# One product for B u, four groups' y beside each other on TensorE's columns, and B turned a layer earlier

## The chip, the cores and the metric

The kernel runs on one core of a Trainium2 chip. The metric is the device time of one execution in microseconds (us), the median of three runs. One execution was also taken by the hardware profiler; its trace is what the rows below come from. TensorE is called PE in rows, VectorE DVE, ScalarE ACT, GpSimd POOL, SyncE SP; PEld is TensorE's weight load.

## The reference, cut to what matters

Two blocks run one after the other: a two-layer attention block over 256 latent and 256 context tokens, and then a block with a state-space mixer (S5), a latent attention (MLA) and a feed-forward part. The change touches the S5 mixer and the tables that it needs. There are 64 groups of 16 channels and 64 complex states; the sequence has 272 tokens, and the outputs of the last 258 are used.

```python
b_bar = ((lam_bar - 1.0) / lam)[..., None] * b
bu = jnp.einsum('blgc,gpc->blgp', uf.astype(jnp.complex64), b_bar)
a = jnp.broadcast_to(lam_bar, bu.shape)
_, h = lax.associative_scan(combine, (a, bu), axis=1)   # h_t = lam_bar h_(t-1) + bu_t
y = jnp.real(jnp.einsum('blgp,gcp->blgc', h, c))
y = y + d_skip * uf
g = jax.nn.gelu(y)
out = g * jax.nn.sigmoid(g @ w_glu + b_glu)
```

## The kernel before

Two groups are one step n of 32: their 2 x 64 states fill 128 partitions. Activations lie transposed, channels on partitions and tokens along the free dimension. A float32 product of accuracy is made of three: `mm3` multiplies a high and a low part of the weights (`wh`, `wl`, both float32r) with a high and a low part of the activations. A stream of weight units (`W`, 512 KB each as a rule) feeds everything: SP loads `raw` (three buffers), ACT rounds it to `wh` (L313), DVE makes `wl` (L327), TensorE multiplies 24 times per unit (4 chunks, 2 halves, 3 products). Work that goes beside the stream is written as Python generators that advance at fixed places of a unit, `pre` and `post`; so the order on each engine's queue is fixed when the program is built, and each engine works its queue in that order.

`s5()` is such a generator. It runs beside three stretches of the stream: the input projection of the second block (`in2`, weights `win2`), the heads of the latent attention (`qb_pair`, `kv_pair`, `mla_head`; there the units are short and have plain float32 products), and the output projection `ob`. One step n is: six float32r products `bu` (L464 to L466: `mm3` for the real and the imaginary part, 32 rows of B, 272 columns) into two PSUM banks; on DVE `rotate` (L1776 to L1781: the two products with the table `e`, a sum, a difference and two scans); on POOL two products with `e` (L1784), a sum and a difference (L1785, L1786), result `pr`; and, three steps later (`late`), two float32 products `y` (L1837), each C of 128 x 128 (zero but for 32 columns) times `pr`. A step's trailing products come 32 channels at a time, and four steps share one PSUM bank; after the fourth, `gelu` follows (L1796 to L1809) on DVE and ACT. For each step SP loads `e` (two buffers) and `ct` (four buffers). Once per four steps B is loaded (`bd`), turned by two transposes (`turned_b`, L1816) and split into `bTH` and `bTL`; those take two `pre`/`post` places of their own.

The tables `etab` and `btab` lie in DRAM; `s5_tables()` makes them beside the second layer of the first block (lines 920 to 1038), and must end before the second block's memory is given out.

Of the kernel before, what the change touches and what calls it, by code (L numbers as in the profile page):

```python
# [63 lines left out]
PACE = {"in2": 6, "heads": 2, "ob": 6, "late": 3}  # L64
# [54 lines left out]
def _layout2(i):  # L119
# [43 lines left out]
    ct = np.zeros((32, 128, 2, 128), np.float32)  # L163
    for v, key in enumerate(("c_re_2", "c_im_2")):
        c = i[key][0]
        for gr in range(64):
            n, h = gr // 2, gr % 2
            o = 32 * (n % 4) + 16 * h
            ct[n, 64 * h:64 * h + 64, v, o:o + 16] = c[gr].T
# [75 lines left out]
def program(ctx: ExitStack, tc: tile.TileContext, A, stop=None):  # L245
# [294 lines left out]
    btab = dram.tile([2, 128, 32, 32], F32, name="btab")  # L540
# [346 lines left out]
    def s5_tables():  # L887
# [83 lines left out]
        for i in range(2):  # L971
# [7 lines left out]
            for v, op in enumerate((SUB, ADD)):  # L979
# [7 lines left out]
                P.dma_start(out=btab[v, :, n0:n0 + 16, :].rearrange("p n c -> p (n c)"), in_=o.rearrange("p n g c -> p (n g c)"))  # L987
# [767 lines left out]
    def s5():  # L1755
        yield
        bT = [mt_("bTH", [128, 2, 128], F32R), mt_("bTL", [128, 2, 128], F32R)]
# [8 lines left out]
        def load_b(j):  # L1766
            t = mw.tile([128, 2, 128], F32, tag="bd", name="bd", bufs=1)
            SY.dma_start(out=t, in_=btab[:, :, 4 * j:4 * j + 4, :].rearrange("v p n c -> p v (n c)"))
            return t

        def rotate(n, bu, e):
# [10 lines left out]
            o, o_ = (ring(t, 2 * NT, k).rearrange("p (v t) -> p v t", v=2) for t, k in (("pr0", 3), ("pr", 1)))  # L1782
            for x, w in ((o, co), (o_, si)):
                P.tensor_tensor(out=x, in0=g, in1=w.unsqueeze(1).to_broadcast([128, 2, NT]), op=MUL)  # L1784
# [7 lines left out]
        def gelu(j, yps):  # L1792
            y, w = ring("gy", NQ, 1), ring("gw", NQ, 1)

            def a():
                V.scalar_tensor_tensor(out=y, in0=uF(j), scalar=dsk[:, j:j + 1], in1=yps[:, 14:NT], op0=MUL, op1=ADD)  # L1796
# [16 lines left out]
        def turned_b(bd, tag):  # L1813
            pt = ps_(tag)
            for v in range(2):
                T.transpose(pt[:, v * 128:v * 128 + 128], bd[:, v, :], ident)  # L1816
            yield
            split(bT[0], bT[1], pt[:, :256].rearrange("p (v q) -> p v q", v=2))

        nxt, bd = load(0), load_b(0)  # L1820
        yield
        yield from turned_b(bd, "O")
        bd = load_b(1)
        yield
        while "x" not in R:
            yield
            yield
        late = deque()
        yps = [None]

        def late_y():
            n, c, parts = late.popleft()
            i = n % 4
# [486 lines left out]
```

## Time and profile before

| what | value |
|---|---|
| median of three runs | 2983.74 us (2981.06 to 2984.47) |
| the profiled execution's own time | 2980.39 us |
| its span | 2978.6 us |
| mean granted TensorE clock | 0.97 |
| second layer of the first block, from the tables' start | 1320 to 1766 us of the span |
| first step of S5 to the first products of the heads | 1826.5 to 1939 us |
| the heads | 1939 to 2068 us |
| fourteen units of `ob` with the last five steps of S5 | 2068 to 2139 us |

The profiled execution lies 3.4 us under the median, 1.8 us of its time outside its span. In the tables of stretches below, an engine's figure is the time in which it had an instruction in work; PEclk is the granted TensorE clock as a share of 2.4 GHz (0.5 is its lower level, 1.2 GHz, so 0.89 is a mixture of both levels). A plain float32 matmul has two records in the trace, a float32r matmul one.

### The profile page before, as it was taken

What the parts mean: (1) busy time and instruction counts of PE and PEld (TensorE: products, weight loads), DVE (VectorE), ACT (ScalarE), POOL (GpSimd) and SP (SyncE); (2) the same over time, 40 slices, a digit from 0 to 9 for tenths busy, and PEclk for the clock granted to TensorE, in tenths of its full rate; (3) what the DMA queues carried; (4) which work ended last, traced back from release to release, by engine and by line L of the source; (5) the groups of instructions that cost most, each with busy time, mean ns of one, the idle gap of its engine ahead of it and who ended that gap; (6) DMA issues with size and microseconds to landing.
All of it is one profiled execution on the core that took longest, in us unless ns stands there. A gap on an engine that the chain in (4) does not pass through costs nothing. (4 is left out here: it accounts for less than half of the span.)

```text
span 2978.6 us, 48955 instructions
## 1 busy us (share of the span) xinstructions
PE 2798.6 (94%) x19022; PEld 2530.3 (85%) x19022; DVE 1980.7 (66%) x3709; ACT 1279.2 (43%) x2196; POOL 526.1 (18%) x501
## 2 busy tenths in 40 slices
PE   6999999998999978999998988899999999999998
PEld 2677878887777978899898987866899999999998
DVE  2377667676676588766676887876865555455544
ACT  2444434244442445534345544234354444344443
POOL 0001100001111161100001125655431110011100
PEclk9999999998999989999999999898999999999999
DMA  9754454543446645534433564432455655666554
GB/s 364 259 163 134 120 150 147 171 130 119 121 139 187 220 155 192 174 100 147 141 125 115 161 191 144 132 110 84 144 160 183 183 183 180 186 187 183 182 176 156
DMA packets 176441, 483.97 MB, mean 162 GB/s; under 512 B 20944, under 2 KB 32848, under 8 KB 176208
## 3 DMA queue, kind: packets, MB, share of 16 engines
q1 hardware_dynamic: 171312, 468.62, 50.2%
q0 software_dynamic: 2880, 9.96, 0.9%
q8 instruction: 149, 2.44, 0.3%
q10 hardware_dynamic: 2016, 2.25, 0.2%
q14 instruction: 84, 0.69, 0.1%
HBM read 468.71 MB, written 12.06 MB: 161 GB/s over the span
## 5 line engine op out<-in xcount | busy, mean ns | idle before, releaser
L327 DVE TENSOR_TENSOR wl<-raw,wh 128x1024 fp32r<-128x1024 f32 (+2 forms) x650 | 809.3, 1250 | 440.5 <-ACT wh L313 435.9
L313 ACT CAST wh<-raw 128x1024 fp32r<-128x1024 f32 (+2 forms) x650 | 669.7, 1036 | 918.1 <-PE mm L465 557.1
L464 PE MATMUL mm<-nH,wh 128*128 128x512 f32 (+1 forms) x2048 | 705.5, 344 | 10.6 <-ACT kp L1109 6.7
L465 PE MATMUL mm<-nL,wh 128*128 128x512 f32 (+1 forms) x2048 | 698.0, 341 | 4.5 <-DVE nL L1097 4.5
L466 PE MATMUL mm<-nH,wl 128*128 128x512 f32 (+1 forms) x2048 | 697.0, 340 | 3.2 <-DVE wl L327 3.1
L464 PEld LDWEIGHTS mm<-nH,wh 128*128 128x128 f32 x2048 | 390.5, 191 | 62.0 <-ACT kp L1109 7.1
L465 PEld LDWEIGHTS mm<-nL,wh 128*128 128x128 f32 x2048 | 390.5, 191 | 50.8 <-DVE nL L1097 6.3
L466 PEld LDWEIGHTS mm<-nH,wl 128*128 128x128 f32 x2048 | 389.8, 190 | 50.7 <-DVE wl L327 4.0
L464 PE MATMUL mm<-ZA,wh 128*128 128x258 f32 (+1 forms) x1408 | 400.4, 284 | 5.0 <-DVE oa L1898 5.0
L466 PE MATMUL mm<-ZA,wl 128*128 128x258 f32 (+1 forms) x1408 | 399.8, 284 | 0.0
L465 PE MATMUL mm<-ZB,wh 128*128 128x258 f32 (+1 forms) x1290 | 363.8, 282 | 0.0
L669 DVE SCALAR_TENSOR_TENSOR acc<-mraw,cs,acc 128x512 f32<-128x512 f32 x420 | 295.6, 754 | 45.8 <-DMA mraw<-in_wmod 43.8
L464 PEld LDWEIGHTS mm<-ZA,wh 128*128 128x128 f32 x1408 | 267.4, 190 | 5.2 <-issue 5.2
L466 PEld LDWEIGHTS mm<-ZA,wl 128*128 128x128 f32 x1408 | 267.4, 190 | 0.0
L465 PEld LDWEIGHTS mm<-ZB,wh 128*128 128x128 f32 x1290 | 245.2, 190 | 0.0
L370 PE MATMUL mm<-wh,nH 128*128 128x256 f32 x736 | 212.5, 289 | 6.7 <-ACT nH L1533 3.4
L372 PE MATMUL mm<-wh,nL 128*128 128x256 f32 x736 | 211.0, 287 | 1.6 <-DVE nL L1535 1.5
L371 PE MATMUL mm<-wl,nH 128*128 128x256 f32 x736 | 210.2, 286 | 0.0
L464 PE MATMUL mm<-yH,wh 128*128 128x256 f32 x688 | 193.5, 281 | 0.0
L465 PE MATMUL mm<-yL,wh 128*128 128x256 f32 x688 | 193.5, 281 | 0.0
L466 PE MATMUL mm<-yH,wl 128*128 128x256 f32 x688 | 193.5, 281 | 0.0
L2258 POOL TENSOR_TENSOR v<-v,a 128x256 f32<-128x256 f32 x43 | 59.4, 1381 | 562.8 <-ACT a L2257 549.6
(499 smaller groups left out, 4885.9 us busy)
## 6 DMA issues: line engine op xcount, KB each, us to landing
raw<-in_win SPq DMA_DIRECT2D x266, 512.0 KB, 3.8
raw<-in_wup SPq DMA_DIRECT2D x172, 512.0 KB, 3.7
mraw<-in_wmod SPq DMA_DIRECT2D x288, 256.0 KB, 2.8
raw<-in_wout SPq DMA_DIRECT2D x76, 512.0 KB, 3.9
raw<-in_wda SPq DMA_DIRECT2D x40, 512.0 KB, 3.7
raw<-in_wdb SPq DMA_DIRECT2D x40, 512.0 KB, 4.2
mraw<-in_wmod SPq DMA_DIRECT2D x28, 512.0 KB, 8.1
mraw<-in_wmod SPq DMA_DIRECT2D x10, 1024.0 KB, 11.1
```

The costliest lines, as they stand in the source:

```text
L313: S.copy(out=h[:, :size], in_=self.raw[j][:, :size])
L327: V.tensor_sub(lo[:, :size], r[:, :size], h[:, :size].bitcast(F32))
L370: T.matmul(o, ah, w[i][0], start=(k == 0 and t % 2 == 0), stop=False)
L371: T.matmul(o, ah, w[i][1], start=False, stop=False)
L372: T.matmul(o, al, w[i][0], start=False, stop=(k == nk - 1 and t % 2 == 1 and last and i == len(w) - 1))
L464: T.matmul(out, wh, ah, start=start, stop=False)
L465: T.matmul(out, wh, al, start=False, stop=False)
L466: T.matmul(out, wl, ah, start=False, stop=stop)
L669: V.scalar_tensor_tensor(out=acc, in0=w, scalar=cs[:, k, v:v + 1], in1=acc, op0=MUL, op1=ADD)
L2258: P.tensor_tensor(out=v, in0=v, in1=a, op=MUL)
```

## The change

The change does five things. (1) `y`: C is stored as 128 x 32, and the products of four steps stand together, each writing its own 32 PSUM partitions, one after the other; 258 columns instead of 272. (2) `bu`: the three products of `mm3` become one over 96 stacked rows, high B, high B, low B against high u, low u, high u; both stacks are brought together by DMA (`load` and the new `load_u`), six DMAs a step on SP. (3) B is turned and split in `s5_tables` and written to `btab` as two parts; `turned_b` and its places go. (4) POOL's four operations of a step cover 258 columns. (5) Buffers and the lag: `ct` 7, `pr0` 5, `late` 2.

```diff
-PACE = {"in2": 6, "heads": 2, "ob": 6, "late": 3}
+PACE = {"in2": 6, "heads": 2, "ob": 6, "late": 2}
...
-                P.dma_start(out=btab[v, :, n0:n0 + 16, :].rearrange("p n c -> p (n c)"), in_=o.rearrange("p n g c -> p (n g c)"))
+                yield
+                yield from hold()
+                pt, of = ps_("X"), o.rearrange("p n g c -> p (n g c)")
+                for q in range(4):
+                    T.transpose(pt[:, 128 * q:128 * q + 128], of[:, 128 * q:128 * q + 128], ident)
+                yield
+                hl = [aw.tile([128, 512], F32R, tag="t2", name="bhl", bufs=3) for _ in range(2)]
+                split(hl[0], hl[1], pt)
+                lock["X"] = False
+                for b_, t in zip(range(2), hl):
+                    P.dma_start(out=btab[b_, n0:n0 + 16, :, v, :].rearrange("(q a) c p -> (a c) q p", a=4), in_=t.bitcast(F32).rearrange("p (q s) -> p q s", q=4))
...
-            c = mw.tile([128, 2, 128], F32, tag="ct", name="ct", bufs=4)
+            c = mw.tile([128, 2, 32], F32, tag="ct", name="ct", bufs=7)
             SY.dma_start(out=c, in_=A["ct"][n])
-            return e, c
+            b = mw.tile([96, 2, 128], F32R, tag="bt", name="bt", bufs=2)
+            for i, part in enumerate((0, 0, 1)):
+                SY.dma_start(out=b[32 * i:32 * i + 32].bitcast(F32), in_=btab[part, n])
+            return e, c, b
+
+        def load_u(n):
+            ro, j = 32 * (n % 4), n // 4
+            t = mw.tile([96, NT], F32R, tag="us", name="us", bufs=2)
+            for i, part in enumerate((0, 1, 0)):
+                SY.dma_start(out=t[32 * i:32 * i + 32, :].bitcast(F32), in_=uu[part][j][ro:ro + 32, :].bitcast(F32))
+            return t
...
-                P.tensor_tensor(out=x, in0=g, in1=w.unsqueeze(1).to_broadcast([128, 2, NT]), op=MUL)
+                P.tensor_tensor(out=x, in0=g[:, :, 14:], in1=w[:, 14:].unsqueeze(1).to_broadcast([128, 2, NQ]), op=MUL)
...
         def late_y():
-            n, c, parts = late.popleft()
...
+            four = [late.popleft() for _ in range(4)]
+            yps = ps_("y")
             for v in range(2):
-                T.transpose(pt[:, v * 128:v * 128 + 128], bd[:, v, :], ident)
...
+                for i, (_, c, parts) in enumerate(four):
+                    T.matmul(yps[32 * i:32 * i + 32, :NQ], c[:, v, :], parts[v], start=(v == 0), stop=(v == 1))
+            gelu(four[0][0] // 4, yps)
...
                 for v in range(2):
-                    mm3(bu[v][:, :NT], bT[0][ro:ro + 32, v, :], bT[1][ro:ro + 32, v, :],
-                        uu[0][j][ro:ro + 32, :], uu[1][j][ro:ro + 32, :], True, True)
-            if late and late[0][0] <= n - pace["late"]:
+                    T.matmul(bu[v][:, :NT], b[:, v, :], u, start=True, stop=True)
+            if len(late) >= 4 and late[3][0] <= n - pace["late"]:
                 late_y()
             if n < 31:
                 nxt = load(n + 1)
+                while R["u"] <= (n + 1) // 4:
+                    yield
+                    yield
+                nxt_u = load_u(n + 1)
```

The order moves with it. SP's queue in the input projection, before (`raw` is a weight unit, `e` and `ct` one step's tables):

```order
L1763 DMA ct<-in_ct 128x256
L297 DMA raw<-in_win 128x1024 x2
L1761 DMA e<-etab 128x544
L1763 DMA ct<-in_ct 128x256
L297 DMA raw<-in_win 128x1024
```

and in the changed program (`bt` is the stack of B, `us` that of u):

```order
L1783 DMA us<-ZA 32x272 x3
L296 DMA raw<-in_win 128x1024 x2
L1769 DMA e<-etab 128x544
L1771 DMA ct<-in_ct 128x64
L1775 DMA bt<-btab 32x256 x3
L1783 DMA us<-ZA 32x272 x3
L296 DMA raw<-in_win 128x1024
```

What stood behind `e` was one DMA of the step; now seven stand there, and the last three are what TensorE's next `bu` reads.

TensorE's queue where the heads end and `ob` begins (its first products are `mm<-XL,wh`), before; the six `bu` rows are step 25 of S5, and step 26 follows behind the last row:

```order
L2089 MATMUL O<-p_20521,XH 128x256
L2092 MATMUL O<-p,v 128x256 x2
L2145 MATMUL PT<-ident,pm 16x2 x8
L464 MATMUL bu_20539<-ZA,bTH 128x272
L465 MATMUL bu_20539<-ZA,bTH 128x272
L466 MATMUL bu_20539<-ZA,bTL 128x272
L464 MATMUL bu_20540<-ZA,bTH 128x272
L465 MATMUL bu_20540<-ZA,bTH 128x272
L466 MATMUL bu_20540<-ZA,bTL 128x272
L1837 MATMUL y<-pr_20224,ct 128x272 x2
L2152 MATMUL O<-pmT,XH 128x2 x8
```

and in the changed program, where the steps there are 30 and 31, the last two:

```order
L2088 MATMUL O<-p_20777,XH 128x256
L2091 MATMUL O<-p,v 128x256 x2
L2144 MATMUL PT<-ident,pm 16x2 x8
L1850 MATMUL bu_20811<-us,bt 128x272
L1850 MATMUL bu_20812<-us,bt 128x272
L2151 MATMUL O<-pmT,XH 128x2 x8
L1850 MATMUL bu_20870<-us,bt 128x272
L1850 MATMUL bu_20871<-us,bt 128x272
L463 MATMUL mm<-XL,wh 128x258
```

Five steps have left `ob`: the input projection has seventeen steps (0 to 16) instead of fourteen, the heads fifteen (17 to 31) instead of thirteen (14 to 26), and `ob` only the last group of `y`, after its second unit.

DVE's queue at the end of the second layer (`et` and `eb` are the tables' last pieces, `gpo` the first operation behind the layer), before:

```order
L1037 SCALAR_TENSOR_TENSOR et<-et,pw,eb 128x16
L327 TENSOR_TENSOR wl<-raw,wh 128x1024 x2
L1596 TENSOR_TENSOR gpo<-mod_89,postg 128x16
L578 TENSOR_SCALAR rv<-PT 128x2
L1729 TENSOR_REDUCE acc_93<-ZB 128x16
```

and in the changed program:

```order
L326 TENSOR_TENSOR wl<-raw,wh 128x1024
L1044 TENSOR_SCALAR eb<-et,pw 128x64
L1045 TENSOR_SCALAR eb<-et,pw 128x64
L1046 SCALAR_TENSOR_TENSOR et<-et,pw,eb 128x64
L1047 SCALAR_TENSOR_TENSOR et<-et,pw,eb 128x64
L1044 TENSOR_SCALAR eb<-et,pw 128x128
L1045 TENSOR_SCALAR eb<-et,pw 128x128
L1046 SCALAR_TENSOR_TENSOR et<-et,pw,eb 128x128
L1047 SCALAR_TENSOR_TENSOR et<-et,pw,eb 128x128
L1044 TENSOR_SCALAR eb<-et,pw 128x16
L1045 TENSOR_SCALAR eb<-et,pw 128x16
```

The tables end later in the queue: three pieces of the last table stand behind the last `wl` of the layer, where none stood.

## Rows read from the trace of the kernel before

**Rows 1.** The page's head: busy time, share of the span and instructions of each engine.
```profile
PE 2798.6 (94%) x19022; PEld 2530.3 (85%) x19022; DVE 1980.7 (66%) x3709; ACT 1279.2 (43%) x2196; POOL 526.1 (18%) x501
```

**Rows 2.** Stretches: length, busy PE, PEld, DVE, ACT, POOL, clock, DMA share, GB/s.
```profile
1320.00:1766.00 446.00, 425.95 (x3179) 405.18 (x3178) 327.87 (x1022) 208.31 (x376) 48.22 (x69) 0.98 0.46 146
1826.50:1939.00 112.50, 95.83 (x612) 87.46 (x610) 90.99 (x129) 29.75 (x54) 76.86 (x63) 0.89 0.42 131
1939.00:2068.00 129.00, 119.48 (x538) 83.00 (x538) 87.03 (x210) 51.52 (x168) 64.17 (x65) 0.92 0.28 82
2068.00:2139.00 71.00, 63.45 (x415) 58.84 (x414) 63.60 (x86) 20.45 (x29) 41.18 (x32) 0.88 0.50 153
2125.00:2139.00 14.00, 14.00 (x118) 13.95 (x117) 10.70 (x16) 5.68 (x8) 1.72 (x2) 1.00 0.55 165
```

**Rows 3.** TensorE's timeline: start, length, line, tiles; one step's bu, one step's y.
```profile
1827.28 0.28 PE L466 MATMUL bu<-ZA,bTL 32*128 32x272 f32 x1
1827.49 0.40 PE L464 MATMUL y<-XH,wh 128*128 128x272 f32 x1
...
2119.71 1.08 PE L1837 MATMUL y<-pr,ct 128*128 128x272 f32 x4
2120.61 0.36 PE L464 MATMUL mm<-XL,wh 128*128 128x258 f32 x1
```

**Rows 4.** TensorE's timeline in the first block: products of 32 output columns.
```profile
96.18 1.92 PE L706 MATMUL S<-mraw,csq 128*32 128x512 f32 x16
98.04 1.05 PE L717 MATMUL X<-sel,row 128*128 128x2 f32 x8
```

**Rows 5.** Groups by line, 1826.5 to 2139 us: busy, mean ns, idle before.
```profile
L1781 DVE TENSOR_TENSOR_SCAN a<-s5r,a 128x272 f32<-128x272 f32 x64 | 46.5, 768 | 1.1
...
L1776 DVE TENSOR_TENSOR a<-bu,e 128x544 f32<-128x544 f32 x64 | 43.2, 714 | 6.8 <-PE bu L466 6.3 <-PE y L1837 0.2
...
L1777 DVE TENSOR_TENSOR a<-a,a 128x272 f32<-128x272 f32 x32 | 19.8, 620 | 1.1
...
L1778 DVE TENSOR_TENSOR a<-a,a 128x272 f32<-128x272 f32 x32 | 19.0, 593 | 0.0
```

**Rows 6.** SP's timeline: two loads of S5 one behind the other.
```profile
1785.60 0.43 SPq L1761 DMA_DIRECT2D e<-etab  x1
1786.07 0.43 SPq L1763 DMA_DIRECT2D ct<-in_ct  x1
```

**Rows 7.** What SP's queue waited for, 1826.5 to 2139 us: total, times, longest.
```profile
SPq L1763 <- PE y L1837: 65.8, 19, 8.4
SPq L1761 <- POOL pr L1784: 61.8, 24, 5.0
```

**Rows 8.** The tile ct: from a load's issue to its landing.
```profile
DMA to landing us min/median/max: 1.9/2.4/5.1
```

**Rows 9.** POOL's timeline: one step.
```profile
1831.97 3.57 POOL L1784 TENSOR_TENSOR pr<-a,e 128x544 f32<-128x544 f32 x2 [10.22 <-DVE a L1781]
...
1836.34 1.76 POOL L1786 TENSOR_TENSOR pr<-pr,pr 128x272 f32<-128x272 f32 x1
```

**Rows 10.** Tiles pr, raw, PT, bd: durations in ns, min/median/max.
```profile
L1784 POOL TENSOR_TENSOR pr<-a,e x64: 1322/1380/2358, 1832.0 to 2115.8; 128x544 f32<-128x544 f32 x64
L327 DVE TENSOR_TENSOR wl<-raw,wh x34: 1194/1225/2395, 1827.2 to 2137.4; 128x1024 fp32r<-128x1024 f32 x34
L1338 DVE TENSOR_TENSOR ptl<-PT,pth x64: 662/688/693, 217.5 to 1678.3; 128x512 fp32r<-128x512 f32 x64
L1816 PE MATMUL bu<-ident,bd x14: 271/273/332, 1849.4 to 2080.3; 128*128 128x128 f32 x14
```

**Rows 11.** Timelines at the end of the second layer: DVE and SP.
```profile
1768.61 1.23 DVE L327 TENSOR_TENSOR wl<-raw,wh 128x1024 fp32r<-128x1024 f32 x1 [0.28 <-ACT wh L313]
1770.29 0.38 SPq L1626 DMA_DIRECT2D ZB<-in_meta  x1
```

**Rows 12.** TensorE's timeline: the first product of a pair in ob.
```profile
2110.32 0.55 PE L464 MATMUL mm<-XL,wh 128*128 128x258 f32 x1 [4.20 <-DVE ob L1898]
```

More of the change, by code (lines that the diff above doesn't have):

```diff
@@ L539, in program @@
     etab = dram.tile([32, 128, 2, NT], F32, name="etab")
-    btab = dram.tile([2, 128, 32, 32], F32, name="btab")
+    btab = dram.tile([2, 32, 32, 2, 128], F32, name="btab")
     half = cst("half", [128, 2], "half")
@@ L1795, in a @@
             def a():
-                V.scalar_tensor_tensor(out=y, in0=uF(j), scalar=dsk[:, j:j + 1], in1=yps[:, 14:NT], op0=MUL, op1=ADD)
+                V.scalar_tensor_tensor(out=y, in0=uF(j), scalar=dsk[:, j:j + 1], in1=yps[:, :NQ], op0=MUL, op1=ADD)
                 S.activation(out=w, in_=y, func=AF.Square, scale=math.sqrt(0.044715))
@@ L1811, in gelu @@
             todo.extend((a, b, c, d))
-        def turned_b(bd, tag):
-            pt = ps_(tag)
-            for v in range(2):
-                T.transpose(pt[:, v * 128:v * 128 + 128], bd[:, v, :], ident)
-            yield
-            split(bT[0], bT[1], pt[:, :256].rearrange("p (v q) -> p v q", v=2))
-        nxt, bd = load(0), load_b(0)
+        nxt = load(0)
         yield
[L1822 to L1825, printed above, removed]
+        while not R.get("u"):
             yield
             yield
+        nxt_u = load_u(0)
         late = deque()
-        yps = [None]
         def late_y():
-            n, c, parts = late.popleft()
-            i = n % 4
-            if i == 0:
-                yps[0] = ps_("y")
-            for v, p in enumerate(parts):
-                T.matmul(yps[0][:, :NT], c[:, v, :], p, start=(i == 0 and v == 0), stop=(i == 3 and v == 1))
-            if i == 3:
-                gelu(n // 4, yps[0])
-        for n in range(35):
-            if 0 < n < 32 and n % 4 == 0:
-                yield from turned_b(bd, "bu0")
-                if n < 28:
-                    bd = load_b(n // 4 + 1)
-                yield
+            four = [late.popleft() for _ in range(4)]
+            yps = ps_("y")
+            for v in range(2):
+                for i, (_, c, parts) in enumerate(four):
+                    T.matmul(yps[32 * i:32 * i + 32, :NQ], c[:, v, :], parts[v], start=(v == 0), stop=(v == 1))
+            gelu(four[0][0] // 4, yps)
+        for n in range(34):
             if n < 32:
-                e, c = nxt
-                ro, j = 32 * (n % 4), n // 4
+                (e, c, b), u = nxt, nxt_u
                 bu = [ps_("bu0"), ps_("bu1")]
                 for v in range(2):
-                    mm3(bu[v][:, :NT], bT[0][ro:ro + 32, v, :], bT[1][ro:ro + 32, v, :],
-                        uu[0][j][ro:ro + 32, :], uu[1][j][ro:ro + 32, :], True, True)
-            if late and late[0][0] <= n - pace["late"]:
+                    T.matmul(bu[v][:, :NT], b[:, v, :], u, start=True, stop=True)
+            if len(late) >= 4 and late[3][0] <= n - pace["late"]:
                 late_y()
@@ L1868, in s5 @@
             yield
-        while late or todo:
-            if late:
-                late_y()
+        while todo:
             yield
-            if todo:
-                todo.popleft()()
+            todo.popleft()()
             yield
@@ L1910, in f @@
                 S.copy(out=uF(2 * p + m), in_=t[m][:, 14:])
+            R["u"] = 2 * p + 2
         return f
```

11 lines of the change are left out of this document (3 added, 8 removed).

## The prediction

> **What bounds the kernel now.** I read the page's head first: TensorE is in work for 94% of the span [rows 1], so the question in each stretch is what keeps TensorE, and what is next. The stretches come second [rows 2]. The change touches four. In the second layer of the first block TensorE is in work for 425.95 of 446 us at clock 0.98, with DVE at 327.87: TensorE is the bound. In the input projection TensorE shows 95.83 of 112.5 us at clock 0.89, DVE 90.99, POOL 76.86: three engines near their limits, tied by the chain of each step. In the heads TensorE shows 119.48 of 129, DVE 87.03. In the stretch of `ob` DVE has 63.60 of 71 us, TensorE 63.45 at 0.88: dense steps of S5 fill DVE, and once S5 is over (2125 to 2139) TensorE runs at full clock with 14.00 of 14.00. So TensorE's work is worth something in the heads, DVE's in `ob`, and in the input projection the chain counts. The groups by line give that chain's prices [rows 5]; SP's waits and POOL's timeline show how it is closed [rows 7, 9].
>
> **The change part by part.**
>
> *y.* At full clock a step's four records take 0.90 us (2119.71 to 2120.61) [rows 3], four steps 3.6. The changed eight products have 16 records of 32 output columns. The trace of before has that form: 16 records of 512 columns take 1.86 us (96.18 to 98.04) [rows 4]; one after the other, by the `y` row's 0.225 us for 272 columns, they would take 16 x 0.225 x 512/272 = 6.8. So four run beside each other, and 258 columns take 1.86 x 258/512 = 0.94 us. Four steps save 2.7 us of TensorE, eight groups 21 us. The page "TensorEngine Tiling (Array Packing)" of the Trainium skill, Key Properties, states that changing the tiling mode drains TensorE, which speaks against this: there are 16 changes. The nearest row is the change from the 32-row `bu` to `y`, 0.21 us from start to start (1827.28 to 1827.49) [rows 3] where 118 products in 14.00 us stand 0.12 apart [rows 2], so some 0.1 us each. Were each drain a whole recorded product (0.28 [rows 3]), 16 of them would cost 16 x 0.16 = 2.6 us.
>
> *bu.* Six products at 0.12 (14.00/118 [rows 2]) become two: 0.72 to 0.24 us a step, 15 us over 32 steps.
>
> Neither 21 nor 15 is a gain in itself; what follows is by stretch.
>
> *B a layer earlier.* Sixteen transposes go to the second layer, where TensorE is the bound: at most 16 x 0.27 = 4.4 us [rows 10], at least nothing. Four casts on ACT and four differences on DVE (0.69 us by the 128 x 512 row [rows 10], 2.8 in all) lie in DVE's idle quarter [rows 2]; four more DMA issues lie on an idle POOL. I take 3 us, 0 to 5, with a wait or two for `bo`. If DVE were not idle there, its 2.8 us would come on top.
>
> *End of that layer.* By the order, three pieces of the last table now stand behind the last `wl`, some 2.2 us of DVE. Before, that `wl` runs from 1768.61, SP issues the next block's first load at 1770.29 [rows 11]. The load's memory must be free of tables, so it can slide by those 2.2 us, or the landing covers them: 0 to 3, I take 1.5.
>
> *Start of S5.* `bu` of step 0 started as soon as u was split. Now three DMAs carry u to the stack: two issues at 0.47 us pitch ahead of the last (1785.60 to 1786.07) [rows 6] and 1.9 to 2.4 us to land [rows 8], 3.3 us, in which TensorE's queue stands. Range 1 to 5, I take 3.5.
>
> *Input projection, 16 steps' distance instead of 13.* The new chain: `e` has two buffers, so SP's load of `e` for step n+2 waits for POOL's two products of step n; before, SP already waited so 24 times, 61.8 us in all [rows 7], but only `rotate` needed what stood behind it. Now `bt` and `us` stand there, and TensorE's next `bu` needs them. One round, two steps: `rotate` 4.0 us ((43.2+19.8+19.0+46.5)/32 [rows 5]); POOL's two products 3.57 x 516/544 = 3.4 [rows 9]; seven issues ahead of the last `us` at 0.47, 3.3 [rows 6]; landing 2.4 [rows 8]; `bu` 0.4; hand-overs 0.5: 14.0 us, so 7.0 a step, 16 x 7.0 = 112. DVE's own work asks 90.99 + 3 x 4.0 = 103 us. Against it SP's 65.8 us of waits for `y` [rows 7] go, since `ct` has seven buffers; that queue also brings the weights. So the stretch takes 112 to 116 with three more steps in it: I take +2. Bounds: a round with the quickest rows (POOL 2 x 1.32 [rows 10], landing 1.9 [rows 8]) is 12.6, 101 us or, DVE permitting, 106: -6; with a slow POOL (2 x 2.36) and a landing of 3.5 it is 16.5, +20, of which I leave 8 to the slow rival: +12.
>
> *Heads, 15 steps instead of 13.* TensorE loses 13 x (0.72 + 0.90) = 21 us and gets 15 x 0.24 + 4 x 0.94 = 7.4: -14. DVE gets 8, and 95 of 129 is no bound. But the last three steps stand with almost nothing between them (the order at the end of the heads), each two 14 us apart by the chain: some 10 us in which TensorE waits, against 3 us of its own work there. I take +10 for it: -4, with -12 (the tail hidden) and +12 (nothing gained, tail exposed) as ends.
>
> *ob.* Fourteen units stood in 71 us. 118 products in 14.00 us [rows 2] are 0.119 each, 24 per unit: 14 x 2.85 = 40 us. On top: one group of `y`, 1; the wait for POOL's last step, whose four operations end 6.1 us after they start [rows 9], behind only two units, 4; the pairs whose banks wait for DVE, 4.20 us once [rows 12], and the climb of the clock, 6. That is 51: -20, between -15 and -28 (bare 43).
>
> Sum: 3 + 1.5 + 3.5 + 2 - 4 - 20 = **-14 us**. The profiled execution took 2980.39, so 2966.4; the median of the runs lies 3.35 higher, and on that scale I forecast **2970**.
>
> **The rivals.** *Slower: the loads of u and B become the bound.* One mechanism, the round above: POOL's products, `e`, six small DMAs, `bu`. For it: POOL's two products reach 2.36 us each where the median is 1.38 [rows 10], and landings reach 5.1 [rows 8], behind weight units on the same rings. Against: steps stood 8 us apart before. At a round of 16.5 us (8.25 a step) the input projection takes 132 (+20) and the heads, 15 steps, 132 (+3): 3 + 1.5 + 3.5 + 20 + 3 - 20 = +11, **2995**. Slower by over 6 us decides at a round of about 16 us. The idle TensorE would also show a lower granted clock than 0.89.
>
> *No change: DVE and POOL take back what TensorE gives.* The freed time is TensorE's, and the S5 steps move into stretches where DVE and POOL already overlap. `wl` goes from 1194 to 2395 ns and POOL's product from 1322 to 2358 [rows 10], each at its worst about twice as long. If a quarter of the steps' POOL products (some 1 us each, four of sixteen) and of the `wl` are so drawn out, the input projection takes +6, the heads +2 and `ob` -17: 3 + 1.5 + 3.5 + 6 + 2 - 17 = -1, **2983**. The page "GPSIMD Engine Reference" of the Trainium skill, section 1, gives DVE and POOL a shared SBUF interface, with contention when DVE has two SBUF inputs, as these operations have; the spread of these rows agrees with it.
>
> *The columns do not run beside each other.* 16 records then take 16 x 0.225 x 258/272 = 3.4 us instead of 0.94, eight groups 20 us more; 12 of it in the heads and in `ob`, where TensorE is the bound: -14 + 12 = -2, **2982**. The 1.86 us of [rows 4] speak against it.
>
> *More.* The tail is hidden and every stretch falls at its good end: 1 + 0 + 1 - 4 - 10 - 24 = -36, **2948**.
>
> **How the numbers follow.** A difference of over 0.2%, 6 us, is what a measurement of this kernel can tell from none. The forecast's case (-6 to -28) has 0.50, more than that 0.07, no change 0.20, columns in series 0.03, slower 0.20. Faster 0.57, same 0.23, slower 0.20. The range 2955 to 2994 leaves out most of "more" and the upper half of "slower".
>
> **What would show it.** Right: groups of `y` with 16 records in about 1 us; `bu` two records; from the first product of `ob` to the end of its fourteenth unit near 51 us; SP's queue with eight loads a step and TensorE waiting for `us` at step 0 and at the heads' end. Wrong: an input projection over 125 us with TensorE waiting for `us<-ZA` at most steps (slower); a heads stretch still at 129 with POOL and DVE longer per operation (no change); starts of `y` records 0.2 us apart one by one (columns in series); a second layer longer by over 5 us.

## The result

The changed kernel takes 3001.38 us (median of 4 runs, 2997.79 to 3002.91), the kernel before beside it 2984.10 (2981.06 to 2985.93): a ratio of 1.0057, 95% interval 1.0040 to 1.0075. It is slower by some 17 us, where the prediction had it 14 faster. The profiled execution took 3001.99, its span is 3000.2, so 21.6 us more than before; the stretches below share out these 21.6, some 4 more than lie between the medians. The page's head (compare [rows 1]) shows a TensorE with less to do and a longer span:

```profile
span 3000.2 us, 48998 instructions
PE 2783.9 (93%) x18894; PEld 2517.7 (84%) x18894; DVE 1984.5 (66%) x3705; ACT 1278.4 (43%) x2192; POOL 513.2 (17%) x505
```

The stretches of [rows 2] between the same events: second layer from the tables on, the way to S5 (from the first operation of the new block to the first `bu`; before, it was 51.2 us, clock 0.87), input projection, heads, fourteen units of `ob`. Columns as in [rows 2]:

```profile
1319.00:1775.50 456.50, 433.34 (x3201) 411.58 (x3199) 326.99 (x1003) 209.72 (x379) 53.85 (x72) 0.98 0.45 144
1784.90:1842.80 57.90, 41.77 (x281) 39.94 (x281) 41.42 (x64) 27.74 (x57) 26.23 (x26) 0.82 0.43 130
1842.80:1965.30 122.50, 90.89 (x566) 84.86 (x566) 101.86 (x145) 28.24 (x51) 82.56 (x73) 0.81 0.45 134
1965.30:2106.20 140.90, 111.60 (x489) 72.43 (x489) 95.00 (x220) 51.87 (x168) 68.43 (x74) 0.81 0.32 91
2106.20:2160.40 54.20, 49.31 (x364) 47.26 (x365) 36.20 (x50) 18.00 (x22) 13.90 (x14) 0.86 0.49 161
```

| stretch | before | after | difference | forecast |
|---|---|---|---|---|
| second layer with its end | 446.0 | 456.5 | +10.5 | +4.5 |
| way to S5 | 51.2 | 57.9 | +6.7 | +3.5 |
| input projection | 112.5 | 122.5 | +10.0 | +2 |
| heads | 129.0 | 140.9 | +11.9 | -4 |
| `ob`, fourteen units | 71.0 | 54.2 | -16.8 | -20 |

The terms add up to 22.3; the rest of the span gives 0.7 back. Every term is off to the same side. By the first rotation of each step, the input projection now has 16 steps and the heads 15, with one more at the border of `ob`; before it was 13, 14 and 5.

Three parts of a stretch are read from its row: **idle** is the length less TensorE's busy time; **work** is busy time x clock, what it would take at 2.4 GHz; the **clock's loss** is the rest of the busy time (this takes the stretch's mean clock for the busy time, an estimate). In the heads: before 109.9 work, 9.6 loss, 9.5 idle; after 90.4, 21.2 and 29.3. So the work did go, 19.5 us of it. The clock took back 11.6 and waiting 19.8.

Places where TensorE waits, in order of time. In the second layer it waits for `bo` twice, 3.9 us in all; `bo` stands on ACT behind a `wh` that in turn waits for TensorE. Behind the wait its products stand 0.21 us apart where they stood 0.12 apart (waits, then timeline):

```profile
PE X L991 <- ACT bo L986: 3.9, 2, 1.9
1329.30 0.28 PE L371 MATMUL mm<-wh,nL 128*128 128x256 f32 x1
1331.52 0.66 PE L991 MATMUL X<-ident,bo 128*128 128x128 f32 x4 [1.94 <-ACT bo L986]
...
1333.73 0.41 PE L370 MATMUL mm<-wl,nH 128*128 128x256 f32 x1
1333.94 0.41 PE L371 MATMUL mm<-wh,nL 128*128 128x256 f32 x1
```

At S5's start the last split of u is followed on DVE by a `wl`, and SP's loads of u stand behind the weight load that needs this `wl`; from there three issues and their landing (DVE, SP, TensorE). The last row names `ct`, but that load had been issued at 1795.56; what came last is `us`:

```profile
1836.35 1.22 DVE L326 TENSOR_TENSOR wl<-raw,wh 128x1024 fp32r<-128x1024 f32 x1
1838.02 1.87 SPq L1783 DMA_DIRECT2D us<-ZA  x3
1842.76 0.79 PE L1850 MATMUL bu<-us,bt 96*128 96x272 f32 x2 [6.98 <-DMA ct<-in_ct]
```

In the input projection TensorE waits 25.5 us for `us` (waits), and a group of `y` is as quick as was worked out (timeline):

```profile
PE bu L1850 <- DMA us<-ZA: 25.5, 9, 4.9
1879.80 1.08 PE L1842 MATMUL y<-pr,ct 128*32 128x258 f32 x16
1880.81 0.39 PE L463 MATMUL mm<-XH,wh 128*128 128x272 f32 x1
```

In the heads the longest wait shows how one queue reaches another, and what follows it. SP's load of `e` waits for POOL; with the seven loads behind it, it holds a weight unit back (issued 2023.28); ACT's `wh` of that unit waits 7.84 us and stands ahead of the `XH` that TensorE needs; TensorE waits 8.12 us, and then runs 21.7 us at the lower level, 1.2 GHz (timelines of SP, ACT and TensorE; stretches before the wait, of the wait, after it, and after that):

```profile
2018.48 0.34 SPq L1769 DMA_DIRECT2D e<-etab  x1
...
2023.28 0.53 SPq L296 DMA_DIRECT2D raw<-in_wob  x1
2027.17 1.04 ACT L312 CAST wh<-raw 128x1024 fp32r<-128x1024 f32 x1 [7.84 <-DMA raw<-in_wob]
2030.83 1.28 PE L2041 MATMUL mm<-k,XH 128*128 128x272 f32 x2 [8.12 <-ACT XH L2116]
2012.00:2022.50 10.50, 10.30 (x50) 6.75 (x42) 9.71 (x16) 2.85 (x7) 5.32 (x5) 1.00 0.29 91
2022.50:2031.00 8.50, 0.38 (x2) 0.18 (x2) 2.53 (x6) 2.37 (x6) 3.20 (x4) 0.67 0.44 135
2031.00:2052.70 21.70, 21.42 (x48) 11.22 (x48) 12.61 (x38) 9.28 (x32) 7.75 (x8) 0.50 0.17 45
2052.70:2063.00 10.30, 9.60 (x50) 5.01 (x48) 6.67 (x21) 4.34 (x16) 3.56 (x4) 1.00 0.03 8
```

TensorE was busy 10.30 of 10.50 us before the wait and at 1.00; after it 21.42 of 21.70 us at 0.50, which costs half of it, 10.7 us. That the wait of 8 us caused these 10.7 is not shown. In `y_epool`, one of the runs below, TensorE stays even longer at the lower level at the same place, in work for all of 27.30 us, though in the 19 us ahead of it no wait was over 1.8 us (waits, 1985 to 2032 us; the stretch before the last wait, and the stay):

```profile
PE mm L2036 <- ACT P L1235: 1.8, 1, 1.8
PE S L2101 <- DVE k L2103: 1.7, 1, 1.7
1992.20:2000.90 8.70, 8.70 (x36) 5.20 (x36) 6.25 (x13) 4.48 (x13) 2.43 (x4) 1.00 0.23 74
2004.00:2031.30 27.30, 27.30 (x80) 15.64 (x80) 13.20 (x42) 10.96 (x36) 9.18 (x12) 0.50 0.08 23
```

### The profile page after: what moved, and what is told of

Its sections match the earlier page's. It is cut to its first block, busy times and chain, and to the rows that moved or that the text cites. A ratio compares the mean times of both kernels' runs of the same rounds, so it can differ in the third digit from the quotient of the medians.

```text
span 3000.2 us, 48998 instructions
## 1 busy us (share of the span) xinstructions
PE 2783.9 (93%) x18894; PEld 2517.7 (84%) x18894; DVE 1984.5 (66%) x3705; ACT 1278.4 (43%) x2192; POOL 513.2 (17%) x505
## 5 line engine op out<-in xcount | busy, mean ns | idle before, releaser
L369 PEld LDWEIGHTS mm<-wh,nH 128*128 128x128 f32 x736 | 143.1, 194 | 18.5 <-issue 5.9
## 6 DMA issues: line engine op xcount, KB each, us to landing
mraw<-in_wmod SPq DMA_DIRECT2D x10, 1024.0 KB, 11.3
```

The lines of the kernel that those rows point to most:

```text
L369: T.matmul(o, ah, w[i][0], start=(k == 0 and t % 2 == 0), stop=False)
```

## The experiments

Theories at the start: **1**, the losses come from the loads of u and B through SP; **2**, TensorE's saving goes back through the clock while S5's chain sets the pace. Later ones are numbered on from there. Where an expectation counts time at the lower level, it is 2 x (1 - clock) x length of the stretch. All ratios are against the kernel before beside the run:

| run | median us | ratio, 95% interval |
|---|---|---|
| `y_only` | 2978.64 | 0.9992, 0.9978 to 1.0005 |
| `tables_only` | 3005.16 | 1.0080, 1.0060 to 1.0099 |
| `after_ahead` | 3002.35 | 1.0069, 1.0054 to 1.0084 |
| `after_epool` | 2996.73 | 1.0046, 1.0031 to 1.0062 |
| `after_places` | 2999.95 | 1.0050, 1.0031 to 1.0070 |
| `tables_places` | 3017.12 | 1.0119, 1.0090 to 1.0149 |
| `y_bu_twice` | 2992.45 | 1.0030, 1.0012 to 1.0048 |
| `y_heads1` | 2996.81 | 1.0051, 1.0035 to 1.0067 |
| `y_dense` | 3000.27 | 1.0057, 1.0037 to 1.0077 |
| `after_dense` | 3007.34 | 1.0077, 1.0050 to 1.0104 |
| `y_each` | 2976.81 | 0.9977, 0.9963 to 0.9990 |
| `y_epool` | 2981.94 | 0.9988, 0.9977 to 0.9999 |
| `after_each` | 3001.53 | 1.0059, 1.0041 to 1.0078 |
| `y_pair` | 2977.22 | 0.9974, 0.9961 to 0.9987 |
| `y_tables` | 2995.13 | 1.0039, 1.0025 to 1.0054 |

Rows below are stretches, columns as in [rows 2], input projection first where two stand, then heads, then `ob`.

### Which part of the change costs: y_only, tables_only, y_tables

`y_only` is the kernel before with this much of the change (and C stored 128 x 32, `ct` 7, `pr0` 5, POOL over 258 columns, lag 2):

```diff
-            for v, p in enumerate(parts):
-                T.matmul(yps[0][:, :NT], c[:, v, :], p, start=(i == 0 and v == 0), stop=(i == 3 and v == 1))
...
+            for v in range(2):
+                for i, (_, c, parts) in enumerate(four):
+                    T.matmul(yps[32 * i:32 * i + 32, :NQ], c[:, v, :], parts[v], start=(v == 0), stop=(v == 1))
```

> Only the y part of the change in the kernel before: C of 128 x 32, four steps' products on quarters of the columns, POOL's four operations over 258 columns, lag 2; B u stays six products, B is turned in the loop as before, the tables are as before. Theory 1 (the loss sits in the loads of u and B, in the table part and at S5's start): layer 2 and S5's start stay as before (0 +- 1 us); y's TensorE work falls by 21 us, of which the heads give some 8, ob some 4: 2984 - 12 = 2972 us, input projection about 112 us, granted clock there 0.87 or more. Theory 2 (TensorE loses its own saving because it idles for S5's chain on DVE and POOL and is granted the lower level of the clock more of the time): input projection 113 to 118 us at a clock of 0.82 to 0.85, heads 128 or more, 2982 to 2988 us.

```profile
1825.90:1934.30 108.40, 87.72 (x604) 80.25 (x603) 89.48 (x129) 29.33 (x54) 71.99 (x63) 0.87 0.40 124
1934.30:2065.30 131.00, 118.43 (x546) 79.57 (x546) 85.87 (x208) 52.11 (x169) 58.56 (x65) 0.83 0.24 71
2065.30:2134.00 68.70, 58.05 (x412) 53.95 (x413) 61.86 (x86) 19.92 (x28) 38.65 (x33) 0.88 0.50 153
```

Nothing that 0.2% can tell. The input projection gains 4.1 us, `ob` 2.3, the heads lose 2.0: by the three parts 98.3 work (11.6 less than before), 20.1 loss (10.5 more), 12.6 idle (3.1 more). Theory 2 holds in the heads, but not in the input projection, where the clock stays at 0.87.

`tables_only` has the transposes beside the second layer and, in S5, two loads in place of turning:

```diff
-                yield from turned_b(bd, "bu0")
+                bT = bd
                 if n < 28:
                     bd = load_b(n // 4 + 1)
-                yield
```

> Only the part on B in the kernel before: B turned and split beside the second layer, loaded as two parts once per four steps by two DMAs; the two places per four steps for turning go; six products of B u and the old y stay, and nothing is loaded for u. Theory 1: the second layer is longer by the 8 to 10 us seen in the changed kernel (two waits of 2.2 us of the transposes for bo, sixteen transposes, the lower clock behind the waits); S5's start costs nothing; input projection 112 to 116 us with three more steps in it, heads 122 to 128, ob some 12 shorter: 2984 + 9 + 2 - 4 - 12 = 2979 us. Theory 2: input projection and heads together at least 10 us longer than before, 2990 us or more.

```profile
1835.60:1967.40 131.80, 113.11 (x669) 101.29 (x669) 111.65 (x152) 29.46 (x53) 91.02 (x76) 0.87 0.43 130
1967.40:2116.10 148.70, 130.06 (x546) 88.89 (x546) 99.18 (x224) 53.76 (x173) 75.01 (x75) 0.88 0.28 85
2116.10:2163.60 47.50, 46.39 (x357) 45.35 (x357) 28.67 (x43) 17.22 (x20) 7.27 (x9) 0.96 0.49 155
```

The dearest part, and it has no load of u: +19.3, +19.7 and -23.5 us in the three stretches, with 17, 15 and 0 steps in them (by the first rotation, here and below). Theory 1 falls as the main cause.

`y_tables` is both parts, so the change without the stacks.

> The change without the stacks: y four steps at once and B turned beside the second layer, loaded as two parts once per four steps, no loads of u, six products of B u a step. If the stacks (their loads and waits) cost more than the four products a step that they save: S5's start is without the 6.7 us, input projection 115 to 120, heads 136 to 141, total 2990 to 2996. Rival (the stacks pay, and the earlier places and the second layer cost it all): total 3001 or more, since the run with the tables alone took 3005.

```profile
1832.50:1954.60 122.10, 104.69 (x660) 94.05 (x660) 103.38 (x148) 29.70 (x54) 79.77 (x73) 0.85 0.40 120
1954.60:2100.90 146.30, 119.83 (x547) 79.38 (x547) 102.91 (x229) 53.35 (x173) 71.97 (x78) 0.83 0.27 80
2100.90:2147.90 47.00, 45.71 (x364) 44.71 (x365) 29.06 (x42) 17.09 (x20) 7.86 (x10) 0.95 0.51 157
```

2995.13, 11 us over the 2984.21 beside it. With the stacks it is 3001.38, so these cost some 6 us, about what S5's start costs (6.7); the intervals of the two ratios overlap, so by the medians alone the 6 us are not told from none. The parts do not add up: the tables alone cost 21 us, with the y part beside them 11, and the y part alone nothing that can be told. The heads were expected at 136 to 141 and took 146.3, the input projection at 115 to 120 and took 122.1. That is without any load of u, against 122.5 with it: the 25.5 us for which `bu` waits for `us` cost nothing that another wait would not have cost.

### The loads: after_ahead, after_epool

In `after_ahead` the stacks are loaded two steps ahead, before `e`:

```diff
-                nxt = load(n + 1)
-                while R["u"] <= (n + 1) // 4:
-                    yield
-                    yield
-                nxt_u = load_u(n + 1)
+                if n < 30:
+                    while R["u"] <= (n + 2) // 4:
+                        yield
+                        yield
+                    ahead.append((load_u(n + 2), load_bt(n + 2)))
+                nxt = load(n + 1)
```

> The changed kernel with the loads of the stacks of u and B issued two steps ahead instead of one and ahead of e, in the same two buffers each. Theory 1: the 25 us for which TensorE's bu waits for us in the input projection go (to under 8 us), the input projection falls from 122.5 to 112 to 115 us and its clock rises from 0.81 to 0.86 or more, heads fall by 3 to 8 us: 3001 - 13 = 2988 us. Theory 2: S5's chain on DVE and POOL sets the pace: waits change their name, the input projection stays within 3 us of 122.5 and the total within 5 us of 3001.

> The changed kernel with e loaded by POOL's queue instead of SP's: what e waits for, POOL's two products of two steps before, stands ahead of it on the same queue, so SP waits for POOL no more, and neither the stacks nor weight units stand behind such a wait. Theory 1: SP's waits for POOL (15.5 us in the input projection, 49.7 in the heads) go, the weight unit that kept TensorE waiting 8.1 us in the heads comes earlier: heads 141 to 128 us, input projection 122 to 117: 3001 - 16 = 2985 us; against it stands what an issue costs POOL (0.5 to 0.8 us by the btab issues). Theory 2: total within 5 us of 3001.

The edit of the second is one word:

```diff
-            SY.dma_start(out=e, in_=etab[n])
+            P.dma_start(out=e, in_=etab[n])
```

Heads of the two runs:

```profile
1960.30:2105.60 145.30, 113.30 (x489) 73.86 (x488) 98.01 (x226) 52.66 (x170) 71.15 (x76) 0.83 0.33 98
1953.70:2100.50 146.80, 116.49 (x488) 74.97 (x488) 100.22 (x228) 52.65 (x170) 81.12 (x93) 0.80 0.34 98
```

`after_ahead` changes nothing in the total. In the trace TensorE's waits for `us` are gone; the input projection takes 118.4 us, and the heads give it back. `after_epool` takes the input projection to 115.3 and the heads to 146.8. The loads are worth 4 to 7 us in the one stretch, not 13 to 16 in the sum. Since TensorE idles 30.3 us of the heads even without SP's waits for POOL, the held-back weight unit shown above is one instance, not the cause of the stretch's length. Ahead of the same products (`mm<-k,XH`) TensorE also waits 5.9 us in `tables_only` and 5.2 in `y_tables`, there for `P` from ACT and with no stack to load.

### Where the steps stand: after_places, tables_places, y_heads1

**Theory 3**: the five steps that left `ob` cost more where they went. `after_places` and `tables_places` keep two empty places per four steps; `tables_places` also has two more places ahead of the transposes in the second layer; `y_heads1` is `y_only` with the heads' pace at 1:

```diff
+            if 0 < n < 32 and n % 4 == 0:
+                yield
+                yield
```

> The changed kernel with the two empty places per four steps kept where B used to be turned, so that S5's steps fall on the stretches as in the kernel before (14 in the input projection, 13 in the heads, 5 in ob). Theory 3 (the steps that were moved out of ob cost more where they went, 6 to 10 us each in the input projection and the heads, against 3 to 4.6 in ob): input projection 122.5 to about 112, heads 141 to about 131, ob and what follows 70 to 86: 3001 - 5 = 2996 us or less, 2992 with the y part's gain. Theory 1 (the loads through SP): the input projection keeps over 118 us and the heads over 137 with fewer steps, total 3001 +- 4.

```profile
1839.60:1946.60 107.00, 83.23 (x544) 78.13 (x544) 83.03 (x123) 26.96 (x47) 69.11 (x62) 0.85 0.47 139
1946.60:2080.40 133.80, 112.69 (x484) 74.46 (x484) 85.76 (x206) 51.11 (x166) 59.01 (x65) 0.80 0.30 86
2080.40:2152.50 72.10, 56.13 (x390) 52.99 (x391) 60.44 (x85) 19.75 (x27) 36.89 (x34) 0.82 0.53 160
```

The three stretches move as theory 3 says: 15.5 us less for three steps in the input projection, 7.1 for two in the heads, 17.9 more for five in `ob`, net -4.7. Its prices do not come out: a step is worth 5.2, 3.6 and 3.6 us, so one moved between the heads and `ob` gains nothing. The profiled execution (2994.20) was also the fastest of six, and the medians (3001.4 and 3000.0) do not tell the two kernels apart, where 2996 or less was expected.

> The kernel before with B turned and split beside the second layer (two more places between bo and its transposes than in the change), loaded as two parts once per four steps, and the two places per four steps kept empty in the loop. Theory 3: input projection, heads and ob come back to those of the kernel before (112.6, 129.3, 86.6, each within 4 us), where the run without the places had 131.8, 148.7 and 63.6; the second layer loses the two waits of the transposes for bo (about 4.4 us of the 8.6), the end of the layer grows by 2 to 6: 2984 + 4 + 5 = 2993 us. Rival: the loads of the two parts or the six products beside y cost the time themselves, and input projection and heads stay over 120 and 138 us.

It took 3017.12, 24 us over what was expected and 12 over `tables_only` (the intervals just overlap), so the places gained nothing here. The transposes no longer wait for `bo`, as expected. But the input projection stayed at 121.1 us, over the rival's 120, and the heads at 137.3, just under its 138, with 14, 13 and 5 steps where the kernel before has 13, 14 and 5. By the three parts the heads have the work of before (109.1 us against 109.9), 14.9 of loss against 9.6 and 13.3 of idle against 9.5; here `y` has its old form, so gathering is not all that moves the clock. What makes the stretches longer is open.

> The y part alone with one number changed: an extra place after every step in the heads instead of after every second, so fewer steps stand in the heads and more in ob. Theory 3: a step costs 6 to 10 us in the heads and 3 to 4.6 in ob: with three steps moved heads 131 to 115, ob and what follows 85 to 98: 2979 - 4 = 2975 us. Rival: the heads keep their length, since their own products and softmax set it, and ob only grows: 2985 us or more.

```profile
1935.30:2058.80 123.50, 111.85 (x510) 75.11 (x511) 75.56 (x189) 51.48 (x167) 48.54 (x53) 0.85 0.25 73
2058.80:2152.30 93.50, 67.71 (x448) 62.11 (x449) 75.75 (x103) 19.64 (x27) 54.09 (x44) 0.80 0.37 115
```

Three steps fewer in the heads (10 instead of 13) take 7.5 us from them and put 24.8 us on `ob`, whose DVE fills up. So a step has no fixed price: in this direction 2.5 us in the heads and 8.3 in `ob`, and neither more steps in the heads nor fewer was faster. The 98 us expected for `ob` and what follows was 109.6.

### The clock in the heads: y_bu_twice, y_dense, after_dense, y_each, y_pair, after_each

```diff
-                for v in range(2):
+                for v in (0, 1, 0, 1):
                     mm3(bu[v][:, :NT], bT[0][ro:ro + 32, v, :], bT[1][ro:ro + 32, v, :],
```

> The y part alone, and the six products of B u run twice (the second time over the first, the output is the same): 0.72 us more of TensorE's work a step, which puts back most of the 0.67 us a step that the y part takes out; it waits for nothing and nothing waits for it but rotate. Theory 2 (TensorE's saving in the heads is given back through the clock): the clock in the heads goes from 0.83 back to 0.88 to 0.92, and the heads stay at 129 to 132 us in spite of 9 us more work. Rival: heads 138 us or more at a clock of 0.83, so the saving was real and is lost elsewhere. Total by theory 2 2976 to 2984 us.

```profile
1937.70:2078.80 141.10, 129.83 (x632) 90.92 (x631) 85.74 (x211) 52.40 (x169) 59.45 (x65) 0.85 0.24 67
```

The heads grow by 10.1 us over `y_only` for 10.1 us of added work (14 x 0.72; in both runs the products of B u of 14 steps stand in the stretch), idle 11.3. TensorE's work is on the path there, so the rival holds: the work that `y_only` removed was worth its time, and it was lost elsewhere. What had risen is the clock's loss (20.1 there, 19.5 here, 9.6 before), and work as such does not bring it back.

**Theory 4**: the dense old products had kept the clock up. `y_dense` and `after_dense` add two of that form:

```diff
+                for v in range(2):
+                    T.matmul(bu[v][:, :NT], ident, e[:, v, :], start=True, stop=True)
```

> The y part alone, with two plain float32 products of 128 rows and 128 columns over 272 columns added ahead of each step's B u (identity times e, into the banks that B u then overwrites): 0.9 us more of TensorE's work a step, of the same form and count as the old y products, where the run with B u twice added 0.72 us of products of 32 rows. Theory 4 (the old y products, dense and one pair a step, are what went missing when the clock fell): time at the lower level in the heads back from 45 us to 20 to 30, heads 128 to 135 us in spite of 11.7 us more work, total 2976 to 2988. Rival (any such work only adds itself, as B u twice did): the clock in the heads stays at 0.83, heads 140 us or more, total 2993 or more.

> The changed kernel with the same two products added ahead of each step's B u, in TensorE's queue just ahead of the place where it waits for the stack of u. Theory 4: they run in time in which TensorE waits, and the time at the lower level falls (input projection 46 to under 30 us, heads 53 to under 35): input projection within 4 us of 122.5, heads 130 to 140, total 2990 to 3002 with 29 us more work. Rival: each adds its 0.9 us: input projection 132 us or more, heads 150 or more, total 3015 or more.

Heads of `y_dense`; input projection and heads of `after_dense`:

```profile
1946.40:2090.30 143.90, 132.34 (x604) 88.87 (x602) 86.40 (x211) 52.21 (x169) 59.23 (x65) 0.86 0.24 68
...
1839.00:1960.40 121.40, 98.22 (x627) 86.97 (x628) 99.52 (x144) 27.64 (x50) 82.86 (x73) 0.90 0.46 135
1960.40:2112.50 152.10, 128.01 (x554) 86.10 (x552) 95.03 (x220) 52.32 (x169) 68.82 (x74) 0.83 0.30 85
```

In the heads theory 4 falls: 0.86 and 143.9, 0.83 and 152.1 us. In the input projection of `after_dense` it holds: the clock goes from 0.81 to 0.90 and the stretch is 1.1 us shorter with 14 us more work (16 x 0.9), run in time in which TensorE waited. Whether the form of the products did that, or only that the waits were filled, no run separates; the total was no lower (3007.34).

**Theory 5**: it is the grouping of four steps' `y` into one place. `y_each` and `after_each` do each step's two narrow products by themselves at a lag of three, `y_pair` two steps' at once:

```diff
-                for i, (_, c, parts) in enumerate(four):
+                for i, (_, c, parts) in enumerate(two, i0):
```

> The y part alone, but each step's two products by themselves at a lag of three steps, as before the change: 32 columns on the step's own quarter, nothing beside them, so TensorE's work for y stays at some 0.85 us a step, spread over the steps. It keeps C of 128 x 32 and POOL's 258 columns. Theory 5 (the grouping of four steps' products into one place leaves long places without them, and that is when the clock falls): time at the lower level in the heads 20 to 28 us as before the change, heads 128 to 132, total 2978 to 2986. Rival (the narrow products, whatever their grouping, or something else than y's placing): 38 us or more at the lower level, heads 137 or more, total 2988 or more.

> The y part with two steps' products at once on two quarters instead of four: TensorE's work for y 0.47 us a step, between 0.24 (four at once) and 0.85 (each by itself), and never more than two steps without. Theory 5: time at the lower level in the heads between 15 us (each by itself) and 45 (four at once), near 25; heads 122 to 128; total 2968 to 2977, the fastest of all. Rival: the clock falls as with four at once (40 us or more), heads 130 or more, total 2978 or more.

> The changed kernel with one thing put back: each step's two products of y by themselves on their quarter at a lag of three steps, instead of four steps' at once. TensorE gets 0.65 us a step more to do. Theory 5 (the grouping lets the clock fall in the heads): time at the lower level in the heads from 53 to 30 us or less, heads 141 to 133 or less in spite of 10 us more work, input projection 122.5 +- 4, total 2988 to 2996. Rival (in the changed kernel the clock falls for the waits of S5's denser steps, whatever y's grouping): 45 us or more at the lower level in the heads, heads 145 or more, total 3001 or more.

Heads of `y_each`, `y_pair` and `after_each`:

```profile
1934.30:2062.50 128.20, 117.39 (x540) 76.25 (x539) 85.66 (x211) 51.54 (x168) 59.11 (x64) 0.94 0.25 74
...
1931.40:2062.50 131.10, 114.60 (x540) 76.16 (x539) 85.87 (x209) 51.91 (x169) 58.65 (x65) 0.91 0.24 71
...
1965.00:2109.10 144.10, 119.73 (x489) 72.98 (x488) 96.19 (x223) 52.38 (x171) 69.98 (x75) 0.86 0.33 93
```

| heads of | length | work | clock's loss | idle |
|---|---|---|---|---|
| before | 129.0 | 109.9 | 9.6 | 9.5 |
| `y_each` | 128.2 | 110.3 | 7.0 | 10.8 |
| `y_pair` | 131.1 | 104.3 | 10.3 | 16.5 |
| `y_only` (four at once) | 131.0 | 98.3 | 20.1 | 12.6 |
| changed kernel | 140.9 | 90.4 | 21.2 | 29.3 |
| `after_each` | 144.1 | 103.0 | 16.8 | 24.4 |

With the steps where they were, the granted clock follows the grouping: 0.94, 0.91, 0.83. Other executions bear it out: the mean clock of the whole span was 0.966 to 0.973 in the ten of `y_each`, 0.966 to 0.970 in the nine of `y_pair` and 0.962 to 0.968 in the ten of `y_only`. The profiled ones are the ends of these ranges for `y_each` and `y_only` (0.973 and 0.962), so one profile of each may show the difference too large. The length hardly moves (`y_pair` was expected at 122 to 128 us and took 131.1): what work is taken out comes back as loss or as idle time. In the changed kernel ungrouping brings the clock from 0.81 to 0.86, but 12.6 us more work eat that, and 24.4 us of idle stay: there the rival holds as well, and the total is the same (3001.53).

`y_each` and `y_pair` are faster than both kernels, by about a quarter of a per cent over the kernel before. Their medians do not tell them apart, and their intervals overlap that of `y_only`. `y_epool` was another try for speed:

> A try at a faster version: the y part alone with e loaded by POOL's queue, where POOL's products that e's buffer waits for stand ahead of it. In the changed kernel that took 7 us from the input projection and gave 6 back in the heads. If SP's waits for POOL keep weight units away from TensorE: input projection 108 to 103, heads within 3 of 131, total 2970 to 2975. Rival: an issue costs POOL's chain as much as the wait did, total 2978 +- 3 or more.

It took 2981.94, its rival's figure.

## Why the prediction was wrong

**The heads, 16 us off.** The step that failed is "TensorE's work is worth something in the heads", used as if the clock and the idle time stood still. The work fell by 19.5 us by the rows, more than the 14 that was worked out. Its price was right too, where the clock and the idle time hardly change: 10.1 us added cost 10.1 (`y_bu_twice`). But the clock's loss rose by 11.6 us and idle by 19.8, so the stretch came out at +11.9, the very end of the range given for it. `y_only` against `y_each` shows that four steps' `y` in one place moves the clock; `y_tables` and `tables_only` show idle of 26.5 and 18.6 us when 15 steps stand in the heads. The 10 us for the steps at the heads' end were the only wait that was counted. There TensorE waits 5.8 us (timeline); most of the 29.3 us of idle lies earlier, in waits spread over the stretch, 8.12 us the longest:

```profile
2099.03 2.17 PE L2151 MATMUL O<-pmT,XH 16*128 16x2 f32 x16 [1.99 <-DVE XL L475]
2104.99 0.79 PE L1850 MATMUL bu<-us,bt 96*128 96x272 f32 x2 [3.80 <-DMA us<-ZA]
```

**The input projection, 8 off.** "16 x 7.0 = 112" is the mis-sized term: 16 steps took 122.5, or 7.7 each, inside the range given (-6 to +12). By the three parts the work fell from 85.3 to 73.6 us, the loss rose from 10.5 to 17.3 and idle from 16.7 to 31.6. The round as it was worked out does not set the length alone: its loads are worth 4 to 7 us (`after_ahead`, `after_epool`), and 17 steps without loads of u took 122.1. DVE was in work for 101.86 of the 122.5 us; which order of waits sets the rest is not shown.

**The second layer, 6 off.** "At most 16 x 0.27" holds for the transposes (four groups like that of 0.66 us). "A wait or two for `bo`" was named and taken as nearly free. In the changed kernel two waits of 2.2 us from product to product and the lower clock behind the first would make up most of the rest, but the waits as such are not the cause. In `tables_places` they are gone and TensorE waits longer for `P` instead (5.3 us near the tables' start, against 3.0); from the `wl` at that start to the layer's last product it takes 454.4 us, the changed kernel 456.0, the kernel before 446.4. Nor is the size steady: over this distance the nine profiled programs with the transposes there took 451.5 to 457.8 us, the eight without 443.1 to 447.8. What lengthens the layer besides the transposes is open. At the end of the layer, from the last product's start to the next block's first, the distance went from 3.25 to 5.61 us: 2.4, within the 0 to 3; up to the operation at which the stretch ends, 0.8 of it is left.

**S5's start, 3 off.** The issue and landing took 4.7 us (1838.02 to 1842.76), not 3.3; and the issues stood behind a weight load that needed a `wl`, which the step had left out.

**`ob`, 3 off.** 54.2 us against 51: the direction and nearly the size were right.

**Right**: four narrow products run beside each other, 16 records in 1.08 us, and the next product starts 1.01 us after the group (0.94 worked out). The Trainium skill's "TensorEngine Tiling (Array Packing)", Key Properties, states that a change of the tiling mode drains TensorE; on the way out of the group that is at most these 0.07 us, if the 0.94 holds. The rival with the columns in series (3.4 us a group) is excluded. The slower rival had the sign and nearly the time (2995), but by luck: its loop of loads costs 4 to 7 us in the input projection, where it had 20, and the stacks as a whole some 6; its 132 us for the heads do not follow from its own round (15 x 8.25 is 124). By `tables_only` and `y_tables` the larger part is the turning of B a layer earlier with the steps that it moves; how that splits into places, waits and clock is not shown. The contention of DVE and POOL was not tried by a run of its own: POOL's products kept their length (median 1304 ns, longest 2292, against 1380 and 2358 [rows 10]), but `wl` did not beside S5, 1837 ns in the mean where 24 of them took 1523 before (groups by line, 1842.8 to 2122 us):

```profile
L326 DVE TENSOR_TENSOR wl<-raw,wh 128x1024 fp32r<-128x1024 f32 x21 | 38.5, 1837 | 9.0 <-ACT wh L312 9.0
```

That is 21 x 0.31 = 6.6 us more on DVE, at a place where it has little to spare. It does not set the length of the input projection: in `y_tables` 17 of them took 1527 ns in the mean there, and the stretch was as long (122.1 us; groups by line, 1832.5 to 1954.6 us):

```profile
L326 DVE TENSOR_TENSOR wl<-raw,wh 128x1024 fp32r<-128x1024 f32 x17 | 26.0, 1527 | 17.2 <-ACT wh L312 17.2
```

## What to carry to other kernels

Work taken from an engine whose clock follows what it does is a gain only if the clock stays, so read work, clock's loss and idle apart in each stretch. Short products gathered into one place gave back in the clock what they saved in work (`y_only`); spread over the places they kept the clock, for a gain too small to tell from the gathered ones. Freeing places in a hand-laid schedule moves everything behind them, so ask first in which stretch a step is cheapest. Putting the empty places back is no sure repair: it changed nothing that the medians tell in the changed kernel, and the kernel with the tables alone was no faster for it (3017.12 us against 3005.16). Idle time and the clock's loss of a stretch have to be counted for all its steps, and not only where a wait stands out in the order.

## What the runs showed of the hardware

The granted clock in the heads went 0.94, 0.91, 0.83 as the same narrow products came one, two or four steps at a time, and neither 0.72 us of products of 32 rows a step nor 0.9 us of full float32 products brought the last one to more than 0.86. In the input projection, where the full products ran into waits, they brought 0.81 to 0.90. The Trainium skill's "TensorE: Matmul & The Clock Gate", Part 1, says that a monitor sets the clock by how busy TensorE has lately been; the wait of 8 us, with a clock of 1.00 ahead of it and 0.50 behind it, agrees. Two stays at the lower level do not follow from that sentence: the 21.70 us behind this wait, of which TensorE was busy for 21.42, and the 27.30 us of `y_epool`, busy for all of them, behind 8.70 busy us of 8.70 at 1.00 and a wait of 1.8. That the grouping alone moves the clock was not expected either, and what tips it in the heads stays open.
